# Hybrid conv and S5 block on one core: early activation table and TensorE work, broadcasts in transpose mode, another order for the last tile

## The chip, the core and the metric

The kernel runs as one program on one core of a Trainium2 chip. The metric is the device time of one execution in microseconds; three executions are shown. The core has TensorE (matmuls, PE in the profile; its weight loads are PEld), VectorE (DVE), ScalarE (ACT), GpSimd (POOL) and SyncE (SP), whose queue issues all transfers here. Each engine works through its own list in order; semaphores tie the lists together.

## What is computed

One decoder layer on a 1024 x 1024 float32 input, cut to what matters here:

```python
h = rms_norm(x, pre_g)
proj = h @ w_in                       # conv_a, conv_b, z_c, u_s, z_s, g_c, g_s
cu = ca * sigmoid(cb)
cu = causal_depthwise_conv(cu, conv_w, conv_b)          # 31 taps
cu = silu(layer_norm(cu, conv_ln_g, conv_ln_b))         # over the 1024 channels
conv_out = (cu * silu(z_c)) @ w_conv_out
y = gelu(s5_mimo(u_s, ...))                             # 32 groups, scan over time
y = y * sigmoid(y @ w_glu + b_glu)
ssm_out = (y * silu(z_s)) @ w_ssm_out
merged = sigmoid(g_c) * conv_out + sigmoid(g_s) * ssm_out
x_out = x + rms_norm(merged @ w_out, post_g)
```

## The kernel before

Activations lie with channels on partitions and the 1024 tokens along the free axis, in tiles of 128 x 1024. Each large product is done in three passes for accuracy: weights and activations are split into a high and a low part (`wh`, `wl`, `xh`, `xl`), and high x high, high x low and low x high are added up in PSUM. One output tile of a product over 1024 channels is therefore 8 x 3 x 2 = 48 matmuls of 128 x 512. ScalarE makes the high part, VectorE the low part.

**Start.** The product for u_s (`usp`, L852) begins on x that is not yet normalised: for each k-tile ScalarE multiplies x with the gain column (`gcol`) into `xh` and VectorE makes `xl` (L142, L143). The row scales are worked out beside it: ScalarE squares eight x tiles with a running sum (`xin`, L155), VectorE adds the epsilon, GpSimd raises to the power -0.5 (`r8t`, L159, 128 x 8). To use the scales along the free axis, `x_spread` (L163) spreads each of the eight columns of `r8t` over 128 columns and multiplies by the identity on TensorE into `rb`. That stands between the passes of k-tile 6 of `usp`. ScalarE copies it to `rbc`, with which x and the u_s results are scaled afterwards.

**Middle.** A list `seq` fixes the order of the products: `cb`/`ca` pairs feed the convolution, `gc`, `zc`, `zs`, `gs` are gates, `glu`, `so`, `co` the products of the two branches. Around them a planner (class `Clock`) places the rest while the program is built: every k-step of a product advances a clock by 1.296, and tasks written as generators (`yield cost, delay`) are taken up when their due time and VectorE's planned free time have come. The planned times set only the order in each engine's list. Tasks are the S5 branch, the convolution on VectorE (`conv_taps`, L539), per channel tile the transposes `lnp` with statistics `st` (`ln_stat`, L578 and L582), and `ln_chain`: after the eighth tile's statistics it forms the LayerNorm scale and shift per token (`lnr8`), spreads both over 128 columns by TensorE (`lnr`, `lnm`, L609), and then for each of eight tiles VectorE multiplies and adds (L622, L623), ScalarE applies Silu (L624), and VectorE multiplies by the reloaded z tile `zcr` (L617). In between ScalarE evaluates the gates: `gst` (L962) is the Sigmoid of a `gs` product and frees the PSUM buffer that holds it; `mm` products have two such buffers, the transposes have two of another tag (`aux`).

**End.** `out_k` (L1028) forms the output for eight groups of 128 tokens. `out_tail` squares the result on ScalarE with a running sum (L1043), multiplies it with the post gain on VectorE (L1044), forms the scale (L1047, L1048, GpSimd's power L1051), and adds x (L1055). The last group is done in two halves of 512.

Of the kernel before, what the change touches and what calls it, by code (L numbers as in the profile page):

```python
# [8 lines left out]
F32 = mybir.dt.float32  # L9
# [4 lines left out]
RMS_EPS = 1e-6  # L14
# [21 lines left out]
def tile_hybrid_block(  # L36
# [43 lines left out]
    def PS(name, tag):  # L80
        return ps.tile([128, 1024], F32, tag=tag, name=name)
# [25 lines left out]
    V.memset(mhalf, -0.5)  # L107
    V.memset(halfpi, math.pi / 2)

    xraw = {}  # L110

    def load_xt(k):
# [47 lines left out]

    def x_spread(rb):
        for t in range(8):
            PE.matmul(rb[:, t * 128:(t + 1) * 128], lhsT=r8t[:, t:t + 1].to_broadcast([128, 128]), rhs=ident,  # L163
                      start=True, stop=True)
        rbc = T("rbc")
        A.activation(out=rbc, in_=rb, func=AF.Copy)
        return rbc
# [404 lines left out]
    stat_left, ln_done = [8], [False]  # L572

    def ln_stat(c):
        yield 0.0, 3.5
        p = PS(f"lnp{c}", "aux")
        for t in range(8):
            PE.transpose(p[:, t * 128:(t + 1) * 128], acc[c][:, t * 128:(t + 1) * 128], ident)  # L578
        clk.now += 0.9
        yield 0.0, 2.0  # L580
        for t in range(8):
            V.bn_stats(out=st8[:, t, c, :], in_=p[:, t * 128:(t + 1) * 128])  # L582
            if t % 4 == 3:
                yield 0.9, 0.0
        stat_left[0] -= 1
        yield 0.0, 0.0
# [7 lines left out]
    def ln_chain():  # L594
# [11 lines left out]
        spread = [PS(f"ln{n}", "aux") for n in "rm"]  # L606
        for i, p in enumerate(spread):
            for t in range(8):
                PE.matmul(p[:, t * 128:(t + 1) * 128], lhsT=lnr8[:, i, t:t + 1].to_broadcast([128, 128]),  # L609
                          rhs=ident, start=True, stop=True)  # L610
        clk.now += 3.6
        zload(0)
        zload(1)
        yield 0.0, 3.0
# [112 lines left out]
    def js(j):  # L727
        return slice(j * 512, (j + 1) * 512)
# [72 lines left out]
    dmt = T("dmt")[0:16, 0:512].rearrange("p (g h) -> p g h", g=32)  # L801
    clk.now = clk.dve = 0.0
    usp = {m: PS(f"usp{m}", "aux" if m == 2 else "mm") for m in range(3)}
    for k in range(2):
        x_raw(k)
        us_split(0, k, 2)
# [226 lines left out]

    xo = {}

    def out_tail(pj, t):
        o = T(f"o{t}")
        q = T(f"q{t}")
        n = 1024 // len(pj)
        ssq = small.tile([128, 2], F32, tag="ossq", name=f"ossq{t}")  # L1040
        for i, p in enumerate(pj):
            s = slice(i * n, (i + 1) * n)
            A.activation(out=q[:, s], in_=p, func=AF.Square, accum_out=ssq[:, i:i + 1])  # L1043
            V.tensor_tensor(out=o[:, s], in0=p, in1=pog[:, s], op=ALU.mult)  # L1044
        v = small.tile([128, 1], F32, tag="ov", name=f"ov{t}")
        if len(pj) > 1:
            V.tensor_tensor(out=v, in0=ssq[:, 0:1], in1=ssq[:, 1:2], op=ALU.add)  # L1047
        V.tensor_scalar(out=v, in0=v if len(pj) > 1 else ssq[:, 0:1], scalar1=1.0 / 1024, scalar2=RMS_EPS,  # L1048
                        op0=ALU.mult, op1=ALU.add)
        r = small.tile([128, 1], F32, tag="rstd", name=f"orstd{t}")  # L1050
        G.tensor_tensor(out=r, in0=v, in1=mhalf[:, 0:1], op=ALU.pow)  # L1051
        xt = xo.pop(t)
        for i in range(len(pj)):
            s = slice(i * n, (i + 1) * n)
            V.scalar_tensor_tensor(out=o[:, s], in0=o[:, s], scalar=r, in1=xt[:, s], op0=ALU.mult, op1=ALU.add)  # L1055
            nc.sync.dma_start(out=ov[t][:, s], in_=o[:, s])
# [18 lines left out]
    for j in range(2):  # L1075
        for k in range(8):
            out_k(pl[j], 7, k, (j,))
    out_tail([pl[j][:, js(j)] for j in range(2)], 7)


VERBOSE = False
NT = 21
WRAW = 2
WHL = 2

_INS = ["x", "xt", "w_us", "w_in", "w_co", "w_glu", "w_so", "w_out", "pre_g", "post_g", "conv_w", "chan",
        "bglu", "lam", "bmat", "cmat", "dmat", "ident", "cst", "iota"]
# [67 lines left out]
```

## Time and profile before

| | us |
|---|---|
| median of three runs | 835.36 (834.99 to 835.5) |
| profiled execution | 834.89 |
| its span | 833.1 |
| TensorE matmuls busy | 816.3 (98%) |
| TensorE weight loads busy | 678.2 |
| VectorE busy | 622.6 (75%) |
| ScalarE busy | 279.4 (34%) |
| GpSimd busy | 26.4 (3%) |

A row of the timeline gives start and duration in microseconds, engine, line, operation, what it writes and reads, and how many like it were merged; in brackets stands how long the engine had been idle before and what ended that. Buffer numbers are left out of names. A matmul's duration contains its way through the array, so the pace of TensorE is read from one start to the next, not from durations. Waits of engines that nobody waits for cost nothing.

### The profile page before, as it was taken

To read this page: it belongs to the slowest core of one execution; us is meant where nothing else is said; L and a number is where in the kernel's file an instruction comes from. 1 tells how busy PE (TensorE), PEld (TensorE's weight loads), DVE (VectorE), ACT (ScalarE), POOL (GpSimd) and SP (SyncE) were. 2 spreads that over 40 slices of the span, in tenths; PEclk is the share of its full clock that TensorE was granted. 3 is DMA by queue.
4 is the path that set the end of the run, shared out by engine and by line. 5 is a ranking of instruction groups with operands and counts; after the bars stand their busy time and mean duration, and the time that the engine had idled before them with its cause. 6 is when DMAs were issued, how large, how long until landed. Compare 5 with 4: busy or idle time off the path is not lost.

```text
span 833.1 us, 9759 instructions
## 1 busy us (share of the span) xinstructions
PE 816.3 (98%) x3856; PEld 678.2 (81%) x3856; DVE 622.6 (75%) x902; ACT 279.4 (34%) x301; POOL 26.4 (3%) x26
## 2 busy tenths in 40 slices
PE   6999999999999999999999999999999999999996
PEld 5888888888888888888878888888878788888885
DVE  4689899896998899998989779397594644442242
ACT  5771624455325534323321131222254311122121
POOL 3400000000000000000000000000100000000010
PEclk9999999999999999999999999999999999999999
DMA  9703533533333112111112213122351644424142
GB/s 338 285 27 127 152 100 87 143 105 91 102 90 110 55 51 89 51 50 52 39 39 76 89 39 104 48 89 89 127 190 63 227 152 151 151 75 178 51 177 101
DMA packets 35180, 90.77 MB, mean 109 GB/s; under 512 B 8304, under 2 KB 13040, under 8 KB 35136
## 3 DMA queue, kind: packets, MB, share of 16 engines
q1 hardware_dynamic: 35136, 90.17, 32.2%
q8 instruction: 30, 0.49, 0.2%
q14 instruction: 14, 0.11, 0.0%
HBM read 65.90 MB, written 18.87 MB: 102 GB/s over the span
## 4 chain that ended last, share of the span: by engine, by line
PE 76%; DVE 16%; issue 3%; ACT 2%; DMA 2%; POOL 1%; SPq 0%; DVEq 0%; POOLq 0%; ACTq 0%
PE pgc L738 11%; PE pco L738 10%; PE po L1028 10%; PE pgs L738 9%; PE pcb L738 8%; PE pzc L738 8%; PE pca L738 8%; DVE pp L539 6%; PE pso L738 4%; DVE acc L539 3%; PE usp L871 1%; PE pgl L738 1%; DMA xt<-in_xt_dram 1%; DMA xin<-in_x_dram 1%; POOL spt L227 1%
## 5 line engine op out<-in xcount | busy, mean ns | idle before, releaser
L539 DVE SCALAR_TENSOR_TENSOR pp<-ext,cw,pp 128x512 f32<-128x512 f32 x232 | 165.6, 745 | 9.9 <-ACT pp L530 9.8
L539 DVE SCALAR_TENSOR_TENSOR acc<-ext,hs,acc 128x512 f32<-128x512 f32 x120 | 89.3, 744 | 0.0
L1028 PE MATMUL po<-wox,mgh 128*128 128x512 f32 x192 | 52.3, 389 | 0.0
L1028 PEld LDWEIGHTS po<-wox,mgh 128*128 128x128 f32 x192 | 36.0, 188 | 7.5
L738 PE MATMUL pgs<-xh,wh_gs 128*128 128x512 f32 x128 | 39.6, 391 | 1.2 <-ACT gst L962 1.2
L515 ACT ACTIVATE ext<-ext 128x1179 f32<-128x1179 f32 x8 | 9.5, 1191 | 92.7 <-DVE ext L514 92.7
L738 PE MATMUL pgc<-xh,wh_gc 128*128 128x512 f32 x128 | 40.6, 398 | 0.0
L738 PE MATMUL pca<-xh,wh_ca 128*128 128x512 f32 x128 | 40.1, 395 | 0.0
L738 PE MATMUL pzc<-xh,wh_zc 128*128 128x512 f32 x128 | 39.9, 393 | 0.0
L1000 DVE TENSOR_TENSOR sgr<-pco,sgr 128x1024 f32<-128x1024 f32 x8 | 9.8, 1224 | 40.1 <-PE pco L738 40.1
L738 PE MATMUL pca<-xh,wl_ca 128*128 128x512 f32 x128 | 39.6, 390 | 0.0
L1044 DVE TENSOR_TENSOR o<-po,postg 128x1024 f32<-128x1024 f32 (+1 forms) x9 | 10.0, 1106 | 39.6 <-ACT q L1043 39.6
L738 PE MATMUL pco<-cuh,wl_co 128*128 128x512 f32 x128 | 39.5, 390 | 0.0
L738 PE MATMUL pcb<-xh,wh_cb 128*128 128x512 f32 x128 | 39.5, 390 | 0.0
L738 PE MATMUL pca<-xl,wh_ca 128*128 128x512 f32 x128 | 39.5, 389 | 0.0
L738 PE MATMUL pgc<-xl,wh_gc 128*128 128x512 f32 x128 | 39.5, 390 | 0.0
L738 PE MATMUL pzc<-xh,wl_zc 128*128 128x512 f32 x128 | 39.5, 389 | 0.0
L738 PE MATMUL pzc<-xl,wh_zc 128*128 128x512 f32 x128 | 39.5, 389 | 0.0
L738 PE MATMUL pgc<-xh,wl_gc 128*128 128x512 f32 x128 | 39.5, 389 | 0.0
L738 PE MATMUL pgs<-xl,wh_gs 128*128 128x512 f32 x128 | 39.4, 389 | 0.0
L738 PE MATMUL pco<-cuh,wh_co 128*128 128x512 f32 x128 | 39.4, 389 | 0.0
L738 PE MATMUL pcb<-xl,wh_cb 128*128 128x512 f32 x128 | 39.4, 389 | 0.0
(267 smaller groups left out, 1799.9 us busy)
## 6 DMA issues: line engine op xcount, KB each, us to landing
xt<-in_xt_dram SPq DMA_DIRECT2D x8, 512.0 KB, 6.1
xin<-in_x_dram SPq DMA_DIRECT2D x8, 512.0 KB, 9.8
wr_cb<-in_w_in_dram SPq DMA_DIRECT2D x8, 512.0 KB, 3.4
wr_ca<-in_w_in_dram SPq DMA_DIRECT2D x8, 512.0 KB, 3.3
wr_gc<-in_w_in_dram SPq DMA_DIRECT2D x8, 512.0 KB, 3.7
gc_scratch<-gct SPq DMA_DIRECT2D x8, 512.0 KB, 2.7
wr_zc<-in_w_in_dram SPq DMA_DIRECT2D x8, 512.0 KB, 3.3
zc_scratch<-zct SPq DMA_DIRECT2D x8, 512.0 KB, 2.6
```

Source lines behind the costliest of these rows:

```text
L227: G.tensor_tensor(out=r[:, g_], in0=ebase2[:, g_], in1=a[:, g_], op=ALU.pow)
L515: A.activation(out=ext[:, :, 0:3, 1:132], in_=ext[:, :, 4:7, 0:131], func=AF.Copy)
L539: V.scalar_tensor_tensor(out=o, in0=src(e, r), scalar=w, in1=o, op0=ALU.mult, op1=ALU.add)
L738: PE.matmul(p[:, js(j)], lhsT=lhs[:, ks], rhs=rhs(k, j), start=st, stop=sp_)
L871: PE.matmul(usp[3][:, js(j)], lhsT=lhs[:, ks], rhs=rhs[:, k, js(j)], start=st, stop=sp_)
L1000: V.tensor_tensor(out=sgt, in0=p, in1=sgt, op=ALU.mult)
L1028: PE.matmul(p[:, js(j)], lhsT=lhs[k][:, s], rhs=rhs[k][:, js(j)], start=st, stop=sp_)
L1044: V.tensor_tensor(out=o[:, s], in0=p, in1=pog[:, s], op=ALU.mult)
```

## The change

- A one-column ScalarE copy to `scrap` stands first in ScalarE's list; it reads only a constant, so the activation table is loaded ahead of it and not ahead of the first split.
- VectorE fills a tile `warm`, and TensorE runs three (`WARM`) float32 matmuls on it into a PSUM buffer that nobody reads.
- The broadcasts of `r8t` and of `lnr8` (scale and shift) use TensorE's transpose instead of a product with the identity. The planner counts 1.8 instead of 3.6 for the LayerNorm ones, and the delay ahead of each tile's statistics is 5.0 instead of 3.5. Both move the tasks behind them.
- The last token group uses `out_last`: product with the gain ahead of the square in each half, and the mean of squares added up in two steps, the first on the first half.

```diff
--- before.py
+++ after.py
@@ -107,6 +107,9 @@
     V.memset(mhalf, -0.5)
     V.memset(halfpi, math.pi / 2)
 
+    scrap = small.tile([128, 1], F32, tag="scrap", name="scrap", bufs=1)
+    A.activation(out=scrap, in_=halfpi, func=AF.Copy)
+
     xraw = {}
 
     def load_xt(k):
@@ -160,8 +163,7 @@
 
     def x_spread(rb):
         for t in range(8):
-            PE.matmul(rb[:, t * 128:(t + 1) * 128], lhsT=r8t[:, t:t + 1].to_broadcast([128, 128]), rhs=ident,
-                      start=True, stop=True)
+            PE.transpose(rb[:, t * 128:(t + 1) * 128], r8t[:, t:t + 1].to_broadcast([128, 128]), ident)
         rbc = T("rbc")
         A.activation(out=rbc, in_=rb, func=AF.Copy)
         return rbc
@@ -572,7 +574,7 @@
     stat_left, ln_done = [8], [False]
 
     def ln_stat(c):
-        yield 0.0, 3.5
+        yield 0.0, 5.0
         p = PS(f"lnp{c}", "aux")
         for t in range(8):
             PE.transpose(p[:, t * 128:(t + 1) * 128], acc[c][:, t * 128:(t + 1) * 128], ident)
@@ -606,9 +608,8 @@
         spread = [PS(f"ln{n}", "aux") for n in "rm"]
         for i, p in enumerate(spread):
             for t in range(8):
-                PE.matmul(p[:, t * 128:(t + 1) * 128], lhsT=lnr8[:, i, t:t + 1].to_broadcast([128, 128]),
-                          rhs=ident, start=True, stop=True)
-        clk.now += 3.6
+                PE.transpose(p[:, t * 128:(t + 1) * 128], lnr8[:, i, t:t + 1].to_broadcast([128, 128]), ident)
+        clk.now += 1.8
         zload(0)
         zload(1)
         yield 0.0, 3.0
@@ -801,6 +802,11 @@
     dmt = T("dmt")[0:16, 0:512].rearrange("p (g h) -> p g h", g=32)
     clk.now = clk.dve = 0.0
     usp = {m: PS(f"usp{m}", "aux" if m == 2 else "mm") for m in range(3)}
+    warm = T("warm")
+    V.memset(warm[:, 0:640], 0.0)
+    pw_ = PS("warm", "aux")
+    for _ in range(WARM):
+        PE.matmul(pw_[:, 0:512], lhsT=warm[:, 512:640], rhs=warm[:, 0:512], start=True, stop=True)
     for k in range(2):
         x_raw(k)
         us_split(0, k, 2)
@@ -1033,6 +1039,25 @@
 
     xo = {}
 
+    def out_last(pj, t):
+        o, q = T(f"o{t}"), T(f"q{t}")
+        ssq = small.tile([128, 2], F32, tag="ossq", name=f"ossq{t}")
+        v = small.tile([128, 1], F32, tag="ov", name=f"ov{t}")
+        xt = xo.pop(t)
+        for i, p in enumerate(pj):
+            V.tensor_tensor(out=o[:, js(i)], in0=p, in1=pog[:, js(i)], op=ALU.mult)
+            A.activation(out=q[:, js(i)], in_=p, func=AF.Square, accum_out=ssq[:, i:i + 1])
+            if i == 0:
+                V.tensor_scalar(out=v, in0=ssq[:, 0:1], scalar1=1.0 / 1024, scalar2=RMS_EPS, op0=ALU.mult,
+                                op1=ALU.add)
+        V.scalar_tensor_tensor(out=v, in0=ssq[:, 1:2], scalar=1.0 / 1024, in1=v, op0=ALU.mult, op1=ALU.add)
+        r = small.tile([128, 1], F32, tag="rstd", name=f"orstd{t}")
+        G.tensor_tensor(out=r, in0=v, in1=mhalf[:, 0:1], op=ALU.pow)
+        for i in range(2):
+            V.scalar_tensor_tensor(out=o[:, js(i)], in0=o[:, js(i)], scalar=r, in1=xt[:, js(i)], op0=ALU.mult,
+                                   op1=ALU.add)
+            nc.sync.dma_start(out=ov[t][:, js(i)], in_=o[:, js(i)])
+
     def out_tail(pj, t):
         o = T(f"o{t}")
         q = T(f"q{t}")
@@ -1075,13 +1100,14 @@
     for j in range(2):
         for k in range(8):
             out_k(pl[j], 7, k, (j,))
-    out_tail([pl[j][:, js(j)] for j in range(2)], 7)
+    out_last([pl[j][:, js(j)] for j in range(2)], 7)
 
 
 VERBOSE = False
 NT = 21
 WRAW = 2
 WHL = 2
+WARM = 3
 
 _INS = ["x", "xt", "w_us", "w_in", "w_co", "w_glu", "w_so", "w_out", "pre_g", "post_g", "conv_w", "chan",
         "bglu", "lam", "bmat", "cmat", "dmat", "ident", "cst", "iota"]
```

The planner's numbers move work on three engines. On TensorE, the LayerNorm broadcasts stand inside the last `zc` product in the kernel before (the last `pzc`; `pgs` is the `gs` product behind it):

```order
L738 MATMUL pzc_4365<-xh,wh_zc_4313 128x512 x2
L738 MATMUL pzc_4365<-xl,wh_zc_4313 128x512 x2
L738 MATMUL pzc_4365<-xh,wl_zc_4330 128x512 x2
L609 MATMUL lnr<-ident,lnr_99 128x128 x8
L609 MATMUL lnm<-ident,lnr_99 128x128 x8
L738 MATMUL pzc_4365<-xh,wh_zc_4313 128x512 x2
L738 MATMUL pzc_4365<-xl,wh_zc_4313 128x512 x2
L738 MATMUL pzc_4365<-xh,wl_zc_4330 128x512 x2
L738 MATMUL pzc_4365<-xh,wh_zc_4313 128x512 x2
L738 MATMUL pzc_4365<-xl,wh_zc_4313 128x512 x2
L738 MATMUL pzc_4365<-xh,wl_zc_4330 128x512 x2
L738 MATMUL pgs_4466<-xh,wh_gs_4399 128x512 x2
```

and in the changed kernel:

```order
L739 MATMUL pzc_4369<-xh,wl_zc_4338 128x512 x2
L739 MATMUL pzc_4369<-xh,wh_zc_4321 128x512 x2
L739 MATMUL pzc_4369<-xl,wh_zc_4321 128x512 x2
L739 MATMUL pzc_4369<-xh,wl_zc_4338 128x512 x2
L611 MATMUL lnr<-ident,lnr_101 128x128 x8
L611 MATMUL lnm<-ident,lnr_101 128x128 x8
L739 MATMUL pgs_4468<-xh,wh_gs_4399 128x512 x2
L739 MATMUL pgs_4468<-xl,wh_gs_4399 128x512 x2
L739 MATMUL pgs_4468<-xh,wl_gs_4421 128x512 x2
```

They now stand behind all matmuls of that product, twelve matmuls later.

On ScalarE, the same stretch before, from the last rows ahead of the Silus (`acc`) to the Sigmoid `gst` of the next `gs` product and the table load behind it:

```order
L624 ACTIVATE acc_823<-acc_823,chn 128x1024
L624 ACTIVATE acc_1466<-acc_1466,chn 128x1024
L932 ACTIVATE zct_4482<-pzc_4365 128x1024
L624 ACTIVATE acc_2227<-acc_2227,chn 128x1024
L705 ACTIVATE wh_so_4494<-wr_so_4332 128x512
L624 ACTIVATE acc_2590<-acc_2590,chn 128x1024
L624 ACTIVATE acc_2906<-acc_2906,chn 128x1024
L705 ACTIVATE wh_gs_4549<-wr_gs_4417 128x1024
L962 ACT_TABLE_LOAD
L962 ACTIVATE gst_4551<-pgs_4466 128x1024
L624 ACT_TABLE_LOAD
```

and in the changed kernel:

```order
L625 ACTIVATE acc_831<-acc_831,chn 128x1024
L938 ACTIVATE zct_4484<-pzc_4369 128x1024
L706 ACTIVATE wh_so_4493<-wr_so_4340 128x512
L625 ACTIVATE acc_1474<-acc_1474,chn 128x1024
L625 ACTIVATE acc_2235<-acc_2235,chn 128x1024
L625 ACTIVATE acc_2598<-acc_2598,chn 128x1024
L706 ACTIVATE wh_gs_4551<-wr_gs_4423 128x1024
L968 ACT_TABLE_LOAD
L968 ACTIVATE gst_4553<-pgs_4468 128x1024
L625 ACT_TABLE_LOAD
L625 ACTIVATE acc_2914<-acc_2914,chn 128x1024
```

Further on in the changed kernel, with the two last `gst`:

```order
L625 ACTIVATE acc_3322<-acc_3322,chn 128x1024
L625 ACTIVATE acc_3698<-acc_3698,chn 128x1024
L968 ACT_TABLE_LOAD
L968 ACTIVATE gst_4668<-pgs_4583 128x1024
L625 ACT_TABLE_LOAD
L625 ACTIVATE acc_4066<-acc_4066,chn 128x1024
L706 ACTIVATE wh_so_4679<-wr_so_4572 128x512
L968 ACT_TABLE_LOAD
L968 ACTIVATE gst_4717<-pgs_4652 128x1024
L706 ACTIVATE wh_so_4728<-wr_so_4626 128x512
L990 ACTIVATE cuh<-acc_831 128x1024
```

Four Silus instead of five stand ahead of the first `gst`, `wh_so` stands ahead of the second Silu instead of behind the third, and the eighth Silu now stands between the two last `gst`, with a table load on either side of it. On SP the load of the third z tile (`zcr`) moves behind the last store of `zct`.

On TensorE at the end of the fifth `ca` product to be followed by `gs`, the transposes for the statistics of three tiles before:

```order
L738 MATMUL pca_3174<-xh,wh_ca_3129 128x512 x2
L738 MATMUL pca_3174<-xl,wh_ca_3129 128x512 x2
L738 MATMUL pca_3174<-xh,wl_ca_3146 128x512 x2
L578 MATMUL lnp_3239<-ident,acc_2227 128x128 x8
L738 MATMUL pca_3174<-xh,wh_ca_3129 128x512 x2
L738 MATMUL pca_3174<-xl,wh_ca_3129 128x512 x2
L738 MATMUL pca_3174<-xh,wl_ca_3146 128x512 x2
L578 MATMUL lnp_3262<-ident,acc_2590 128x128 x8
L578 MATMUL lnp_3279<-ident,acc_2906 128x128 x8
L738 MATMUL pgs_3288<-xh,wh_gs_3199 128x512 x2
L738 MATMUL pgs_3288<-xl,wh_gs_3199 128x512 x2
```

and in the changed kernel:

```order
L739 MATMUL pca_3182<-xl,wh_ca_3137 128x512 x2
L739 MATMUL pca_3182<-xh,wl_ca_3154 128x512 x2
L580 MATMUL lnp_3247<-ident,acc_2235 128x128 x8
L739 MATMUL pca_3182<-xh,wh_ca_3137 128x512 x2
L739 MATMUL pca_3182<-xl,wh_ca_3137 128x512 x2
L739 MATMUL pca_3182<-xh,wl_ca_3154 128x512 x2
L580 MATMUL lnp_3270<-ident,acc_2598 128x128 x8
L739 MATMUL pgs_3287<-xh,wh_gs_3207 128x512 x2
L739 MATMUL pgs_3287<-xl,wh_gs_3207 128x512 x2
L739 MATMUL pgs_3287<-xh,wl_gs_3227 128x512 x2
L580 MATMUL lnp_3294<-ident,acc_2914 128x128 x8
L739 MATMUL pgs_3287<-xh,wh_gs_3207 128x512 x2
```

The third group of transposes, which had followed the second directly, now stands six matmuls into `pgs`; at the three later tiles the transposes also stand six matmuls later.

## Rows read from the trace of the kernel before

**Rows 1.** The busy line of the profile's page: busy us (share of span) xinstructions

```profile
PE 816.3 (98%) x3856; PEld 678.2 (81%) x3856; DVE 622.6 (75%) x902; ACT 279.4 (34%) x301; POOL 26.4 (3%) x26
```

**Rows 2.** TensorE's waits in the whole span: us in total, times, longest

```profile
PE lnp L578 <- DVE st L582: 0.7, 2, 0.5
```

**Rows 3.** Timeline of the start: start, duration, engine, line, what, count, idle before

```profile
4.31 1.28 ACT L142 ACT_TABLE_LOAD   x1 [4.31 <-DMA gcol<-in_pre_g_dram]
...
5.61 1.15 ACT L142 ACTIVATE xh<-xt,gcol 128x1024 fp32r<-128x1024 f32 x1
...
7.22 2.93 PE L852 MATMUL usp<-xh,wush 128*128 128x512 f32 x6 [7.22 <-ACT wush L132]
...
11.67 1.52 PE L852 MATMUL usp<-xl,wush 128*128 128x512 f32 x6
...
13.03 1.52 PE L852 MATMUL usp<-xh,wush 128*128 128x512 f32 x6
```

**Rows 4.** Timeline, the way to the row scales and their broadcast

```profile
24.33 1.06 ACT L155 ACTIVATE xin<-xin 128x1024 f32<-128x1024 f32 x1 [0.55 <-DMA xin<-in_x_dram]
...
33.24 1.28 DVE L143 SCALAR_TENSOR_TENSOR xl<-xt,gcol,xh 128x1024 fp32r<-128x1024 f32 x1
...
34.75 1.66 POOL L159 TENSOR_TENSOR r8t<-ssq,mhalf 128x8 f32<-128x8 f32 x1 [3.82 <-DVE spt L251]
34.79 1.52 PE L852 MATMUL usp<-xh,wusl 128*128 128x512 f32 x6
...
36.47 2.05 PE L163 MATMUL rb<-ident,r8t 128*128 128x128 f32 x16 [0.15 <-POOL r8t L159]
...
38.27 1.63 PE L852 MATMUL usp<-xl,wush 128*128 128x512 f32 x6
```

**Rows 5.** Timeline, VectorE at two joints with TensorE: after row scaling, ahead of glu

```profile
46.96 1.22 DVE L176 TENSOR_TENSOR xl<-xt,xh 128x1024 fp32r<-128x1024 f32 x1 [2.17 <-ACT xh L175]
...
288.70 4.63 DVE L794 TENSOR_TENSOR yl<-y,yh 128x1024 fp32r<-128x1024 f32 x4 [1.57 <-ACT yh L793]
```

**Rows 6.** Timeline, eight transposes of channel tile 7 and what follows on TensorE

```profile
583.54 1.03 PE L578 MATMUL lnp<-ident,acc 128*128 128x128 f32 x8
...
584.34 0.70 PE L738 MATMUL pzc<-xh,wh_zc 128*128 128x512 f32 x2
```

**Rows 7.** Timeline, LayerNorm broadcasts and the chain to the next free PSUM buffer

```profile
593.97 1.95 PE L609 MATMUL lnr<-ident,lnr 128*128 128x128 f32 x16
...
595.95 1.22 DVE L622 TENSOR_TENSOR acc<-lnr,acc 128x1024 f32<-128x1024 f32 x1 [4.70 <-PE lnr L609]
...
597.45 0.71 PE L738 MATMUL pzc<-xh,wh_zc 128*128 128x512 f32 x2
597.74 1.23 DVE L623 TENSOR_TENSOR acc<-lnm,acc 128x1024 f32<-128x1024 f32 x1 [0.56 <-PE lnm L609]
...
606.71 0.69 DVE L713 TENSOR_TENSOR wl_so<-wr_so,wh_so 128x512 fp32r<-128x512 f32 x1 [0.70 <-ACT wh_so L705]
...
609.83 1.25 ACT L624 ACTIVATE acc<-acc,chn 128x1024 f32<-128x1024 f32 x1 [3.15 <-DVE acc L623]
...
613.35 1.25 ACT L624 ACTIVATE acc<-acc,chn 128x1024 f32<-128x1024 f32 x1 [2.28 <-DVE acc L623]
...
616.86 1.02 ACT L962 ACTIVATE gst<-pgs 128x1024 f32<-128x1024 f32 x1
...
617.93 0.73 PE L738 MATMUL pgs<-xh,wh_gs 128*128 128x512 f32 x2 [1.16 <-ACT gst L962]
...
640.02 1.03 ACT L962 ACTIVATE gst<-pgs 128x1024 f32<-128x1024 f32 x1 [8.59 <-PE pgs L738]
```

**Rows 8.** Timeline, the end of the last tile

```profile
826.36 0.60 ACT L1043 ACTIVATE q<-po 128x512 f32<-128x512 f32 x1 [4.69 <-PE po L1028]
...
827.08 0.69 DVE L1044 TENSOR_TENSOR o<-po,postg 128x512 f32<-128x512 f32 x1 [4.69 <-ACT q L1043]
...
828.17 0.54 POOL L1051 TENSOR_TENSOR orstd<-ov,mhalf 128x1 f32<-128x1 f32 x1 [9.53 <-DVE ov L1048]
```

## The prediction

> **What bounds the kernel now.** I read four views, in this order. The busy line of the page comes first [rows 1]: TensorE's matmuls are busy 816.3 of the span's 833.1 us, no other engine over 75%. Next TensorE's own waits [rows 2]: apart from the 7.22 us before its first matmul [rows 3], its largest is 1.16 us for one PSUM buffer [rows 7], then 0.7 us in two waits at transposes. So the end is set by the sum of TensorE's instructions plus a few short waits, and a saving counts only if it shortens that stream or one of those waits. Third, the timeline of the start and of the row scales [rows 3, 4], which shows who else could hold TensorE back early. Fourth, the same view where the LayerNorm chain feeds back [rows 7] and at the end [rows 8]. Where VectorE is late it was itself released by TensorE: at 46.96 it had idled 2.17 us for ScalarE, at 288.70 1.57 us [rows 5]. A stream that is about 1 us earlier therefore pulls VectorE along at both joints.
>
> The profiled execution took 834.89 us, 1.79 more than its span. The sum is made against it; the median shown, 835.36, is 0.47 higher, and I add that at the end.
>
> **Start: table load and clock.** ScalarE's table load waits for the gain column until 4.31, and the first split starts 1.30 us later, at 5.61; with the table there it may start at 4.31 at the earliest [rows 3]. The first x tile must also have landed, which no row dates more closely than 5.61, so TensorE starts 0 to 1.3 us earlier. From 7.22 to 13.03 it ran three groups of six matmuls; a later group takes 13.03 - 11.67 = 1.36 us, so 5.81 us stand where 4.08 would: 1.73 us lost to starting at half pace, 1.2 instead of 2.4 GHz, after 7.22 us of nothing [rows 3]. The three added matmuls run while the loads do; at worst they end after the first split and take some of the 1.3 back. VectorE's added fill stands ahead of its first use of data. Together TensorE could be 1.30 + 1.73 = 3.0 us ahead.
>
> I put all of it at nothing, because of what is late next. The row-scale broadcast stands in TensorE's queue between the passes of k-tile 6, and everything on TensorE is queued behind it. It needs r8t, which GpSimd ends at 34.75 + 1.66 = 36.41 [rows 4]. TensorE is ready for it at 34.79 + 1.36 = 36.15 now, and would be at 33.1. The chain to r8t does not move: the squares resume at 24.33 when an x load lands, ScalarE and then VectorE's in-order split at 33.24 follow, then GpSimd [rows 4], and none of these waits for TensorE. The loads are issued at the same places, behind VectorE work that itself waits for later x tiles. So TensorE's head start becomes a wait of 36.41 - 33.1 = 3.3 us.
>
> The Trainium skill (ScalarE: Activation LUTs, What ACT_TABLE_LOAD costs) puts a switch of tables at 2.66 us, drain included. The trace has 1.30 from the start of the load to the next activation [rows 3]. By the page the head start would be 4.4 us instead of 3.0 and be lost in the same wait.
>
> **Row-scale broadcast.** Eight full-precision products, 16 records, take 38.27 - 36.47 = 1.80 us of TensorE [rows 4]. Eight transposes of the same size take 584.34 - 583.54 = 0.80 [rows 6]. They stand on the path, since they start when r8t is there: gain 1.0. The nearest rows have a full tile as operand, not a repeated column; bounds 0 (the repeated column costs as now) and 1.1.
>
> **LayerNorm broadcasts.** The same exchange twice: 597.45 - 593.97 = 3.48 becomes 1.6, gain 1.9, bounds 0 and 2.0 [rows 6, 7].
>
> **What moves behind them.** The broadcasts now stand at the end of the last zc product, 12 matmuls or 2.72 us further on in TensorE's order, so in the old run's time they would start at 593.97 + 2.72 = 596.69. What hangs on them is the chain VectorE, ScalarE's Silu, table load, Sigmoid of gst, which frees the PSUM buffer of the next gs product. Before, that chain took 616.86 - 593.97 = 22.89 and TensorE waited 1.16 at 617.93 [rows 7]. Now four instead of five tiles pass ahead of gst: 613.35 - 609.83 = 3.52 less. The transposes are done 1.04 instead of 1.98 after their start (1.03 busy in rows 6): 0.94 less. VectorE's wait for the second broadcast, 0.56, goes, and so does its 0.70 for wh_so, which ScalarE now does ahead of the second tile instead of behind the third [rows 7]. That leaves 17.17: gst starts at 613.86 and TensorE is released 1.07 later, as in the rows, at 614.93. It arrives at 616.77 - 1.88 = 614.89. The wait shrinks from 1.16 to about 0: gain 1.1. If the 0.70 stays, the gain is 0.5; if the chain keeps its old length, TensorE waits 620.65 - 614.89 = 5.8 us, 4.6 more than now. On SP the load of the third z tile moves behind the last store of zc, which ScalarE frees near 602.5 by the same additions; the third tile's gate comes some 7 us later, and if the load took longer, VectorE and all behind it would stand. I take 1.1, since each subtraction is an instruction that is no longer ahead. Two more table loads, 1.30 us each by rows 3, and the eighth tile, 3.52, now stand on ScalarE between the two last gst; ahead of the last one it had idled 8.59 us [rows 7], which covers these 6.1. Without that cover the splits cuh, queued behind it, would be late for the next stage.
>
> **Transposes for the statistics.** Four tiles' transposes stand six matmuls later. The first of them had stood right behind another tile's and waited 0.5 us, the longer of the two waits in rows 2, until VectorE's statistics freed a PSUM buffer; now 1.36 us of matmuls stand between, more than that wait: gain 0.5, bounds 0 and 0.5. Its own statistics slip behind the next tile's convolution, and what they hold is a PSUM buffer that the transposes after next want, so nothing waits for them.
>
> **Last tile.** Before, square and product follow each other: 0.72 us from 826.36 to 827.08, then 1.09 to GpSimd [rows 8]. Now the product goes first, and I let the square wait for it, as the product waited for the square, though neither needs the other's result: both read the same half of PSUM [rows 8]. 0.69 for the product, some 0.05 to hand over, 0.72 for the square, about 0.30 for one small operation instead of two: 1.76 against 1.81. Gain 0.05, bounds -0.2 and 0.7 (both at once).
>
> **Sum.** 1.0 + 1.9 + 1.1 + 0.5 + 0.05 = 4.55. 834.89 - 4.55 = 830.3, or 830.8 beside the median.
>
> **Rivals.** *The clock falls in the new wait.* TensorE would idle 3.3 us ahead of the broadcast. The trace has two such rows: after 1.16 us idle it went on at full pace (two matmuls in 0.73 us), after 7.22 us it began at half pace [rows 3, 7]. 3.3 lies nearer the first. If it falls, the 1.73 us of the start are paid here, and up to 0.8 for the transposes: 830.8 + 2.1 = 832.9. In the Trainium skill, TensorE: Matmul & The Clock Gate (Why this matters for your kernels) counts idle gaps between bursts of matmuls among the things that return the array to its lower clock; by it this rival is the likelier one, and no row here settles a gap of this length. Chance 0.25.
>
> *The head start is kept*: the way to r8t moves with TensorE after all, say because ScalarE's split of the third weight tile, which waits for TensorE, comes earlier. Against it: a load ends ScalarE's idle time after that. 830.8 - 3.0 = 827.8. Chance 0.06.
>
> *The transposes are no faster* because the repeated column costs as it does now: 830.8 + 2.9 = 833.7. For it: no row shows such an operand in a transpose. Chance 0.05.
>
> *Slower: the clock falls in that wait and stays down.* TensorE runs one remaining pass, three passes and the fourth us product at half pace, 1.36 + 4.08 + 10.9 (eight groups of six) = 16.3 us of work, and loses as much again: 830.8 + 16.3 = 847.1. It decides from 4.55 us of work at half pace on; against it the first start regained full pace after two groups [rows 3]. Chance 0.04.
>
> **Numbers.** The forecast has 0.60 and its own range is 829.7 to 831.9 (buffer wait, tail). 829.2 to 833.0 adds most of the clock case and leaves out the kept head start, the slow cases and the edges. A difference under 0.2% (1.7 us) can't be told from none here. Faster: forecast, clock case, head start and little of the fourth, 0.88 after some is left for what I did not see; same 0.08; slower 0.04.
>
> **What would show it.** Right: TensorE starts near 6, at full pace from its second group at the latest, then waits about 3 us for r8t, which still ends near 36.4; rb, lnr and lnm show 8 records each and some 0.8 us; the wait on gst is under 0.7 and the longer wait at lnp is gone. Wrong: matmuls 0.45 us apart after rb (the clock); r8t ending near 33 (the head start kept); 16 records for rb; a wait of over 1.2 us on gst, which would mean that the LayerNorm chain, now started later, has become the bound there.

## The result, and the profile after

The changed kernel takes 831.26 us (median of six executions, 830.1 to 831.91), the kernel before, timed beside it, 835.43 (834.99 to 835.75): ratio 0.995, 95% interval 0.9937 to 0.9962. Timed again later it took 831.44 against 835.36, ratio 0.9959 (0.9946 to 0.9972). The forecast was 830.8. The total is right to 0.5 us, and one of the steps under it is not. One execution of a kernel further down (the held kernel) took 910.23 us at a granted clock of 0.851 and stands in none of the figures.

The profiled execution of the kernel after took 831.63 us, its span is 829.9 (before 834.89 and 833.1). The busy line and TensorE's waits (in total, times, longest), from the page and the view of the waits; three more, of 0.4 us and less, are as long as before:

```profile
PE 818.3 (99%) x3838; PEld 677.4 (82%) x3838; DVE 622.6 (75%) x903; ACT 282.1 (34%) x304; POOL 25.4 (3%) x26
```

```profile
PE rb L166 <- POOL r8t L162: 2.2, 1, 2.2
PE warm L809 <- DVE warm L806: 1.6, 1, 1.6
PE lnp L580 <- DVE st L584: 0.2, 1, 0.2
```

Beside [rows 1, 2]: TensorE is still what bounds the kernel. It has 24 instructions fewer in the broadcasts and 6 more for warming, and is busy for 2.0 us more: the warming runs from 1.65 to 6.93, when TensorE was idle before, and some later instructions took longer, as the rows below show. The wait on gst is gone from the list, the waits at lnp fell from 0.7 to 0.2, and at the top stands a wait of 2.2 us for r8t.

The start, from the timeline (start, duration, engine, line, what, count, idle before), answers to [rows 3]. The rows of one window merge differently in another, so the last pass of the warming and the first matmul of usp are shown by themselves behind the groups that hold them:

```profile
0.73 1.28 ACT L111 ACT_TABLE_LOAD   x1 [0.73 <-PEq L1169]
...
4.31 1.15 ACT L145 ACTIVATE xh<-xt,gcol 128x1024 fp32r<-128x1024 f32 x1 [2.08 <-DMA gcol<-in_pre_g_dram]
...
1.65 5.28 PE L809 MATMUL warm<-warm 128*128 128x512 f32 x6 [1.65 <-DVE warm L806]
6.14 2.17 PE L858 MATMUL usp<-xh,wush 128*128 128x512 f32 x6
8.16 1.53 PE L858 MATMUL usp<-xh,wusl 128*128 128x512 f32 x6
...
6.07 0.86 PE L809 MATMUL warm<-warm 128*128 128x512 f32 x1
6.14 1.02 PE L858 MATMUL usp<-xh,wush 128*128 128x512 f32 x1
```

The table is loaded while ScalarE would idle, and xh starts at 4.31 instead of 5.61, the full 1.30. TensorE starts 7.22 - 6.14 = 1.08 earlier. Its first group takes 8.16 - 6.14 = 2.02, not the 1.36 of a group at full pace, and the second group is at full pace. Nearly all of the 0.66 between them lies ahead of the group's second matmul: the sixth pass of the warming begins only at 6.07, and the first matmul behind it lasts 1.02 where one of its kind lasts 0.39 at full pace; the other five follow 0.23 apart. So here the warming itself is in the way of the first product. All in all the pass ahead of the broadcast starts at 32.64 instead of 34.79: a lead of 2.15 us.

What became of the lead, the same view, answers to [rows 4]; the last row is the first matmul of the fourth us product, and the fence behind it has two rows of the kernel before:

```profile
32.64 1.52 PE L858 MATMUL usp<-xh,wusl 128*128 128x512 f32 x6
...
34.62 1.66 POOL L162 TENSOR_TENSOR r8t<-ssq,mhalf 128x8 f32<-128x8 f32 x1 [3.81 <-DVE spt L253]
...
36.34 1.09 PE L166 MATMUL rb<-ident,r8t 128*128 128x128 f32 x8 [2.17 <-POOL r8t L162]
37.18 2.79 PE L858 MATMUL usp<-xl,wush 128*128 128x512 f32 x6
39.77 1.99 PE L858 MATMUL usp<-xh,wush 128*128 128x512 f32 x6
41.59 1.53 PE L858 MATMUL usp<-xh,wusl 128*128 128x512 f32 x6
...
44.33 0.62 PE L877 MATMUL usp<-xh,wh_us 128*128 128x512 f32 x2
```

```profile
39.74 1.54 PE L852 MATMUL usp<-xh,wush 128*128 128x512 f32 x6
...
43.84 0.61 PE L871 MATMUL usp<-xh,wh_us 128*128 128x512 f32 x2
```

GpSimd ends r8t at 36.28, before at 36.41: that chain did not move, and the lead became a wait. The transposes take 37.18 - 36.34 = 0.84, the products took 1.80. Then two groups take 39.77 - 37.18 = 2.59 and 41.59 - 39.77 = 1.82 instead of 1.36 each: 1.69 us more. Some 0.1 of that stands behind every broadcast (the first group behind it took 39.74 - 38.27 = 1.47 before), so close to 1.6 us are lost. The row of the stretch shows why (stretch, length, then busy time with its count for PE, PEld, DVE, ACT and POOL, the granted clock, the transfer engines' share, GB/s):

```profile
37.20:40.80 3.60, 3.60 (x12) 2.86 (x10) 3.42 (x13) 1.18 (x2) 0.00 (x0) 0.53 0.33 116
```

The granted clock is 0.53 from 37.2 to 40.8, the lower of its two levels (1.2 GHz) but for the edges; ahead of it TensorE had idled 2.17 us. So in this execution TensorE stands 44.33 - 43.84 = 0.49 us later than before at the fourth product, with the cheaper broadcast in it.

The statistics' transposes and the LayerNorm chain, answering to [rows 2, 6, 7]; the first fence is the kernel before:

```profile
422.78 1.09 PE L578 MATMUL lnp<-ident,acc 128*128 128x128 f32 x8 [0.17 <-DVE st L582]
424.36 1.09 PE L578 MATMUL lnp<-ident,acc 128*128 128x128 f32 x8 [0.49 <-DVE st L582]
...
616.16 0.61 PE L738 MATMUL pso<-y2h,wl_so 128*128 128x512 f32 x2
```

```profile
423.20 1.09 PE L580 MATMUL lnp<-ident,acc 128*128 128x128 f32 x8 [0.15 <-DVE st L584]
...
596.40 1.04 PE L611 MATMUL lnr<-ident,lnr 128*128 128x128 f32 x8
597.27 1.04 PE L611 MATMUL lnm<-ident,lnr 128*128 128x128 f32 x8
...
610.10 1.25 ACT L625 ACTIVATE acc<-acc,chn 128x1024 f32<-128x1024 f32 x1 [2.28 <-DVE acc L624]
...
613.61 1.03 ACT L968 ACTIVATE gst<-pgs 128x1024 f32<-128x1024 f32 x1
...
614.03 0.61 PE L739 MATMUL pso<-y2h,wl_so 128*128 128x512 f32 x2
614.68 0.74 PE L739 MATMUL pgs<-xh,wh_gs 128*128 128x512 f32 x2
...
636.82 1.03 ACT L968 ACTIVATE gst<-pgs 128x1024 f32<-128x1024 f32 x1 [3.56 <-PE pgs L739]
```

The two broadcasts take 598.06 - 596.40 = 1.66 us (the next matmul starts at 598.06) instead of 3.48. The fourth Silu is the last ahead of gst, which starts at 613.61, 17.21 us after the first broadcast (17.17 and 613.86 were worked out). Between the last pair of pso, 0.45 long, and the next gs product stand 614.68 - 614.03 - 0.45 = 0.20 us; counted the same way it was 617.93 - 616.16 - 0.45 = 1.32 before, and not the 1.16 of [rows 7], where idling counts from the pair's modelled end. The idle time ahead of the last gst is 3.56, before 8.59: the cover held.

The last tile, answering to [rows 8]:

```profile
822.75 0.39 PE L1034 MATMUL po<-wox,mgl 128*128 128x512 f32 x1
...
823.18 0.69 DVE L1048 TENSOR_TENSOR o<-po,postg 128x512 f32<-128x512 f32 x1 [3.79 <-PE po L1034]
823.90 0.60 ACT L1049 ACTIVATE q<-po 128x512 f32<-128x512 f32 x1 [4.70 <-DVE o L1048]
...
824.93 0.54 POOL L1055 TENSOR_TENSOR orstd<-ov,mhalf 128x1 f32<-128x1 f32 x1 [9.46 <-DVE ov L1053]
```

The square starts when the product ends: one still waits for the other. GpSimd starts 824.93 - 822.75 = 2.18 after the last matmul starts, before 828.17 - 825.93 = 2.24 by this row and [rows 8]:

```profile
825.93 0.39 PE L1028 MATMUL po<-wox,mgl 128*128 128x512 f32 x1
```

The account of this execution from TensorE's starts: +0.49 up to the fourth product; then up to lnr -0.78 (596.40 against 593.97 + 2.72 = 596.69, which is -0.29 in all); from there to the last matmul -2.89 (825.93 became 822.75, -3.18 in all); the tail -0.06. The sum, -3.24, is the change of the span.

### The profile page after: what moved, and what is told of

Its sections match the earlier page's. It is cut to its first block, busy times and chain, and to the rows that moved or that the text cites. A ratio compares the mean times of both kernels' runs of the same rounds, so it can differ in the third digit from the quotient of the medians.

```text
span 829.9 us, 9728 instructions
## 1 busy us (share of the span) xinstructions
PE 818.3 (99%) x3838; PEld 677.4 (82%) x3838; DVE 622.6 (75%) x903; ACT 282.1 (34%) x304; POOL 25.4 (3%) x26
## 4 chain that ended last, share of the span: by engine, by line
PE 78%; DVE 14%; DMA 3%; issue 2%; ACT 2%; SPq 0%; POOL 0%; DVEq 0%; POOLq 0%; ACTq 0%
PE pgc L739 11%; PE pgs L739 11%; PE pco L739 11%; PE po L1034 10%; PE pzc L739 8%; PE pcb L739 8%; PE pca L739 8%; DVE pp L541 6%; PE pso L739 5%; DVE acc L541 3%; DMA xt<-in_xt_dram 1%; PE usp L877 1%; DMA xin<-in_x_dram 1%; PE pgl L739 1%; PE ep L415 1%
## 5 line engine op out<-in xcount | busy, mean ns | idle before, releaser
L739 PE MATMUL pco<-cul,wh_co 128*128 128x512 f32 x128 | 39.4, 389 | 0.0
L739 PE MATMUL pgs<-xh,wl_gs 128*128 128x512 f32 x128 | 39.4, 389 | 0.0
L739 PE MATMUL pcb<-xh,wl_cb 128*128 128x512 f32 x128 | 39.4, 389 | 0.0
```

The costliest lines, as they stand in the source:

```text
L739: PE.matmul(p[:, js(j)], lhsT=lhs[:, ks], rhs=rhs(k, j), start=st, stop=sp_)
```

## Experiments

Theory W: the head start ends in the wait for r8t, and the low clock behind the broadcast comes of that wait. Its rivals are named in each expectation; the main ones are N (the clock falls for another reason) and H (the head start brings something). Four kernels went first, beside the kernel before (835.2).

**The broadcast later in TensorE's order.** The changed kernel with one line altered:

```
-            if k == 6 and n_ == 5:
+            if k == 7 and n_ == 2:
                 rbc = x_spread(PS("rb", "aux"))
```

The lines below it in the same block, which set the planner's account of VectorE and record the row scalings, move with it.

> The row-scale broadcast stands six pairs of matmuls (2.72 us) later in TensorE's order, in k-tile 7 instead of 6; all else is as in the changed kernel. Theory W (the head start of 2.15 us ends in the wait for r8t, and the lower clock that follows comes of that wait): TensorE gets to the broadcast at 34.0 + 2.72 = 36.7, after r8t at 36.3, so no wait over 0.2 us, granted clock 1.00 from 36 to 42, and the fourth us product starts near 40.5 instead of 44.33. The 3.8 us are kept unless VectorE's split chain (idle 2.8 us at 47.45) becomes late: 827.5 to 829.5, best guess 828.3. Rival N (the lower clock comes of the transposes or of chance, not of the wait): the clock still falls to 0.5 behind the broadcast, and only the wait goes: about 829.2. Rival D (VectorE's chain sets the time here anyway): waits of the same length appear at the convolution products, 831.

Measured 835.07 (833.78 to 836.14), ratio 0.9997 (0.9988 to 1.0006): the whole gain gone. At the broadcast all went as W said: no wait, clock 1.00, fourth product at 40.55. The rows show where it was lost, on TensorE and on VectorE (39.80 in the kernel after for the second row):

```profile
57.63 1.22 PE L739 MATMUL pcb<-xh,wl_cb 128*128 128x512 f32 x2 [5.14 <-DVE wl_cb L714]
...
44.58 4.86 DVE L172 SCALAR_TENSOR_TENSOR xt<-xt,gcol,rbc 128x1024 f32<-128x1024 f32 x4
```

The planner fills VectorE with S5 chores until the row scalings are recorded, so the 2.72 us that they came later let it put some 4 us of chores (40.44 to 44.58) ahead of them. wl_cb came late, TensorE waited 5.14 us, and behind that wait the clock fell as well: the pair that starts at 57.63 takes 1.02 us instead of 0.45. No theory had this in its numbers: the edit moved more than the broadcast.

**Without the warming matmuls** (the fill and the three matmuls left out, the early table load kept).

> The changed kernel without the three warming matmuls and their fill; the early table load stays. Theory W: the first matmul starts near 6.1 at half pace and three groups take 5.8 us, so about 0.8 us less of lead than with warming: the wait for r8t is 1.3 instead of 2.17 us. If a wait of that length leaves the clock alone (as 1.16 us did before), the time is 831.3 - 1.7 = 829.6; if the clock falls as well, 831.3. Rival N (clock falls by chance or by the transposes): 831.3 whatever the wait. Rival H (warming is what brings the gain): 833 or more.

Measured 830.36 (829.75 to 830.78), ratio 0.9941 (0.9929 to 0.9954). The row of the broadcast and that of the clock:

```profile
36.99 1.09 PE L166 MATMUL rb<-ident,r8t 128*128 128x128 f32 x8 [2.00 <-POOL r8t L162]
```

```profile
37.20:40.80 3.60, 3.60 (x21) 3.09 (x20) 3.38 (x18) 1.85 (x2) 0.00 (x0) 1.00 0.10 24
```

r8t ended at 36.94 in this execution, so the wait was 2.00 and not 1.3, and yet the clock stayed at 1.00. A wait of 2.0 us can thus pass without a fall, so neither W nor N is decided here. Rival H is out: nothing is lost without warming.

**Transposes and planner numbers alone** on the kernel before, with neither of the two head edits nor the new tail.

> The kernel before with the transposes for both broadcasts and the two planner numbers alone: no early table load, no warming, the old tail. Theory W: the broadcast waits only the 0.3 us that it waited before, the clock stays at 1.00, and the time is the kernel before less 1.0 (rb), 2.9 (LayerNorm) and 0.7 (statistics), 835.4 - 4.6 = 830.8 or less, so not slower than the changed kernel. Rival H (the early table load and the warming are worth something): 832 or more. Rival N: the clock falls behind rb here too, 832.4.

Measured 830.57 (830.16 to 832.1), ratio 0.9947 (0.9934 to 0.9961): not told apart from the whole change. This part carries all of the gain; 835.2 - 830.57 = 4.6 stands beside a forecast of 4.5 for it.

**The two head edits alone** on the kernel before.

> The kernel before with the early table load and the three warming matmuls alone. Theory W: 2 us of lead turn into a wait of 2.2 us for r8t, and the matmuls behind it run at half pace for 1.7 us of loss (a little more, as the eight broadcast products are in it): 835.4 + 1.7 to 2.5 = 837 to 838 where the clock falls, 835.4 where it doesn't. Rival H (head start of use): 833.3. Rival N (the transposes bring the clock down): 835.4, clock at 1.00 behind rb.

Measured 836.14 (834.54 to 837.31), ratio 1.0011 (1.0002 to 1.002): slightly slower than the kernel before. In the profiled execution:

```profile
36.04 2.66 PE L166 MATMUL rb<-ident,r8t 128*128 128x128 f32 x16 [1.90 <-POOL r8t L162]
...
38.36 2.72 PE L860 MATMUL usp<-xl,wush 128*128 128x512 f32 x6
40.91 1.53 PE L860 MATMUL usp<-xh,wush 128*128 128x512 f32 x6
```

```profile
37.20:40.80 3.60, 3.60 (x15) 3.12 (x14) 3.28 (x12) 1.02 (x1) 0.00 (x0) 0.53 0.41 125
```

The wait and the fall are there with products instead of transposes, so the transposes are not their cause. The loss is 38.36 - 36.04 - 1.80 = 0.52 in the products and 40.91 - 38.36 - 1.47 = 1.08 in the group behind them, 1.6 in all. The size expected, 1.7 to 2.5 on the median, was too much: of eleven executions two kept a mean granted clock of 0.998 or more and took 834.54 and 835.31.

These four left open whether the wait itself brings the clock down, and whether the head start can be had at all. Four more kernels:

**The wait filled with work:** eight matmuls of no use between the pass and the broadcast.

```
             if k == 6 and n_ == 5:
-                rbc = x_spread(PS("rb", "aux"))
+                rb = PS("rb", "aux")
+                for _ in range(8):
+                    PE.matmul(rb[:, 0:512], lhsT=h[:, kk[0]], rhs=xh[:, k, 0:512], start=True, stop=True)
+                rbc = x_spread(rb)
```

> The changed kernel with eight more matmuls of a us weight (0.227 us each at full pace, 1.8 us in all; their result is overwritten) between the second pass of k-tile 6 and the broadcast, so TensorE works through the wait for r8t instead of idling. Theory W (the low clock behind the broadcast comes of TensorE idling there): idle time ahead of rb under 0.5 us, granted clock 1.00 from 36 to 42, the fourth us product starts at 42.7 instead of 44.3, and the time is 831.3 - 1.4 = 829.9 (the executions of the changed kernel in which the clock does not fall gain nothing, so less than the full 1.7). Rival N (the clock falls for another reason): the fall stays, and the eight matmuls cost nothing or up to 0.3 us: 831.3.

Measured 830.15 (829.66 to 831.05), ratio 0.9941 (0.9929 to 0.9953), all five executions at a mean granted clock of 0.997 or 0.998.

```profile
36.54 1.09 PE L166 MATMUL rb<-ident,r8t 128*128 128x128 f32 x8 [0.54 <-POOL r8t L162]
37.38 1.62 PE L858 MATMUL usp<-xl,wush 128*128 128x512 f32 x6
38.84 1.52 PE L858 MATMUL usp<-xh,wush 128*128 128x512 f32 x6
```

Same point of the program, same wait for r8t, but TensorE works through it: the group behind it takes its 1.46, no fall. The median is 1.3 us below that of the changed kernel timed beside it (831.44), with eight matmuls more whose result is thrown away. The two ranges overlap (829.66 to 831.05 against 829.77 to 833.73), so the gain in time is likely and not certain; N would have it only by chance.

**The broadcast later, VectorE's account held.**

```
             if k == 6 and n_ == 5:
+                clk.dve = max(clk.dve, clk.now + 1.5) + 4 * 1.28
+            if k == 7 and n_ == 2:
                 rbc = x_spread(PS("rb", "aux"))
-                clk.dve = max(clk.dve, clk.now + 1.5)
+                held = clk.dve
                 for k_ in range(4):
                     x_scale(k_, rbc)
+                clk.dve = held
```

> The broadcast six pairs of matmuls later in TensorE's order, as in the cover run, but with the planner's account of VectorE left as in the changed kernel, so that VectorE's and ScalarE's orders do not change. Theory V (the cover run lost its 3.8 us because the planner used the later broadcast to put 4 us of S5 chores ahead of the four row scalings on VectorE, which made wl_cb late): the scalings start at 39.8 to 40.3 instead of 44.6, ScalarE's copies of the us products start near 40, wl_cb is split near 52.5, TensorE's wait for it is under 1 us instead of 5.1, and the time is 827.6 to 829, best guess 828.3: the fastest so far. Rival D (VectorE's stream cannot be earlier here whatever its order): the wait for wl_cb stays at 3 us and over, and the time is 831 or more.

Measured 828.89 (four executions, 828.55 to 830.16), ratio 0.9927 (0.9915 to 0.994).

```profile
53.45 0.73 PE L739 MATMUL pcb<-xh,wl_cb 128*128 128x512 f32 x2 [0.61 <-DVE wl_cb L714]
```

```profile
40.40 4.87 DVE L172 SCALAR_TENSOR_TENSOR xt<-xt,gcol,rbc 128x1024 f32<-128x1024 f32 x4
...
52.18 1.22 DVE L714 TENSOR_TENSOR wl_cb<-wr_cb,wh_cb 128x1024 fp32r<-128x1024 f32 x1
```

Theory V by its numbers: scalings at 40.40, wl_cb at 52.18, its wait 0.61 instead of 5.14. Six us lie between this kernel and the first of this section, and the two differ only in where the chores stand on VectorE.

**The planner's old numbers** (3.5 and 3.6 put back, transposes kept).

> The changed kernel with the planner's two old numbers (3.5 for the statistics' transposes, 3.6 for the broadcasts); the transposes stay. By the terms of the prediction the wait on the gst buffer (1.1) and the longer wait at the statistics' transposes (0.5; 0.7 by the trace after) come back: 831.3 + 1.7 = 833.0. Rival P (the placement is worth nothing, the waits went because the transposes are shorter): 831.3, with no wait over 0.4 at pgs or lnp.

Measured 834.06 (832.79 to 835.76), ratio 0.9985 (0.9976 to 0.9993).

```profile
PE lnp L580 <- DVE st L584: 0.7, 2, 0.5
```

```profile
614.74 0.61 PE L739 MATMUL pso<-y2h,wl_so 128*128 128x512 f32 x2
617.00 0.74 PE L739 MATMUL pgs<-xh,wh_gs 128*128 128x512 f32 x2 [1.64 <-ACT gst L968]
```

Both waits are back, and the one on gst, 1.64, is longer than the 1.16 before [rows 7]: TensorE comes to it sooner by more than the shorter broadcasts save on the chain to gst. From start to start it is 617.00 - 614.74 - 0.45 = 1.81, against 0.20 in the changed kernel, and the late group of transposes again stands 1.58 behind the one ahead of it. So of the 3.7 us that the trace of the changed kernel gains here (0.78 and 2.89), the planner's two numbers hold more than half: 1.61 at gst and 0.78 at lnp, 2.4 in all. The two profiled executions, both with the fall, differ by 833.99 - 831.63 = 2.36.

**The changed kernel again.**

> The changed kernel once more, beside the three others of this call. All theories: 830.1 to 831.9. Theory W adds: an execution with a wait of about 2 us for r8t has a granted clock of 0.5 for some 3 us behind the broadcast and the fourth us product at 44 or later, one without has it at 42.7.

Median 831.44 (829.77 to 833.73). Its profiled execution took 830.04:

```profile
36.29 1.09 PE L166 MATMUL rb<-ident,r8t 128*128 128x128 f32 x8 [1.74 <-POOL r8t L162]
...
42.69 0.62 PE L877 MATMUL usp<-xh,wh_us 128*128 128x512 f32 x2
```

```profile
37.20:40.80 3.60, 3.60 (x18) 2.98 (x17) 3.42 (x13) 1.13 (x2) 0.00 (x0) 1.00 0.26 102
```

No fall here, with nearly the same wait, and the fourth product at 42.69 instead of 44.33. The changed kernel's executions look to be of two kinds. Of all twelve, six have a mean granted clock of 0.996 or less and took 831.1 to 833.7 (mean 832.2), six have 0.997 or more and took 829.8 to 831.4 (mean 830.5). The difference, 1.7 us, is near what the two traces show: from rb to the fourth product 44.33 - 36.34 = 7.99 with the fall and 42.69 - 36.29 = 6.40 without, 1.59 more. But only these two of the twelve have a trace, and the mean also holds a low clock that every profiled execution shows behind its last matmul (0.50 from 826.8 on in both). The profiled execution of the head edits alone fell at a mean of 0.997. So the count of six and six is likely, not certain.

Last, whether the length of the wait decides, the tail, and how far the head start carries:

**The broadcast three pairs earlier**, a longer wait (x_spread at `k == 6 and n_ == 2`, the scalings where they were).

> The changed kernel with the broadcast three pairs of matmuls (1.36 us) earlier in TensorE's order, the other engines' orders as they were: TensorE idles about 3.5 us ahead of it instead of 1.7 to 2.2, and all behind it ends 1.36 later. Theory W (the longer TensorE idles there, the surer the clock falls): every execution has the fall, 832.6 (the slower of the two groups of the changed kernel's executions) + 1.4 = 834.0. Rival L (length does not matter): still two groups, 831.6 and 834, median 832.8. Rival N (no link with idling): 831.4 + 1.4 = 832.8 in one group, clock at 1.00.

Measured 832.65 (831.11 to 833.83), ratio 0.9965 (0.9952 to 0.9977).

```profile
36.08 1.09 PE L166 MATMUL rb<-ident,r8t 128*128 128x128 f32 x8 [2.88 <-POOL r8t L162]
36.92 1.64 PE L858 MATMUL usp<-xh,wusl 128*128 128x512 f32 x6
```

W, as I had put it, fails here: the profiled execution (831.16) waited 2.88 us and went on at full pace. Two executions at 0.998 took 831.1, three at 0.996 to 0.997 took 832.7 to 833.8, as rival L has it; the median alone fits N's 832.8 as well. Between 1.7 and 2.9 us the length of the wait does not settle whether the clock falls.

**The old last tile** in the changed kernel (`out_tail` instead of `out_last`).

> The changed kernel with the old last tile (square ahead of product). All theories: same time as the changed kernel within 0.1 us by the trace: GpSimd's power starts 2.24 us behind the last matmul instead of 2.18. Rival B (product and square run together once the product goes first): the old tail is 0.7 us slower, 832.1.

Measured 831.73 (830.14 to 832.46), ratio 0.9961 (0.9947 to 0.9975), the changed kernel's time. By the trace GpSimd starts 823.35 - 821.12 = 2.23 after the last matmul starts, instead of 2.18. Rival B is out.

**The held kernel without warming.**

> The held cover run without the three warming matmuls. Theory W (a head start is worth its length once nothing behind it waits): TensorE gets to the broadcast 0.8 us later than with warming (first matmul at half pace until 10), so 829.1 + 0.8 less the 0.4 to 0.6 us by which the wait for wl_cb shrinks: 829.3 to 829.9. Rival H (warming brings nothing even here, since the wait for wl_cb is what ends last): 829.1, and the wait for wl_cb gone.

Measured 829.54 (828.83 to 829.67), ratio 0.9929 (0.9917 to 0.9942): not told apart from the held kernel with warming. The wait for wl_cb (0.6 in the held kernel) is gone from its waits, so part of the lead that the warming had brought only goes into that wait there.

**The held kernel with wl_cb split one k-tile earlier.**

```
         if k == 1:
             wsplit_h()
-        if k == 2:
             wsplit_l()
```

> The held cover run with the split of wl_cb one k-tile earlier on VectorE (ahead of the third xl). Theory V: the 0.6 us wait for wl_cb goes and nothing replaces it: 829.1 - 0.5 = 828.6, the fastest. Rival D (VectorE's stream ends last whatever its order): another xl or the same split is waited for as long, 829.1.

Measured 827.83 (827.69 to 828.22), ratio 0.9911 (0.9898 to 0.9925): the fastest kernel of the study, 3.4 to 3.6 us below the changed one. wl_cb is split at 49.99, the matmul that waited for it runs at 52.56 without a wait, and the broadcast waits 0.51 us for r8t; no fall in the profiled execution, and a mean granted clock of 0.998 or 0.999 in all four.

## Why the prediction was right, step by step

**Row-scale broadcast**, 1.0: 1.80 - 0.84 = 0.96. The repeated column costs a transpose nothing.

**LayerNorm broadcasts and the wait on gst**, 1.9 and 1.1: 3.48 - 1.66 = 1.82 and, from start to start, 1.32 - 0.20 = 1.12; 2.94 together, 2.89 in the account of starts. That subtracting what no longer stands ahead of gst gave 17.17 us for 17.21 is the best-working step of the text. The run with the old numbers shows that the wait would have grown from 1.16 to 1.64 had the broadcasts not been moved too.

**Statistics**, 0.5: 0.78. The profile put 0.5 down as idle, but from start to start the late group in the kernel before stood 424.36 - 422.78 = 1.58 behind the one ahead of it, 0.78 more than the 0.80 that it takes [rows 6]. An idle figure counts from a modelled end; starts do not.

**Last tile**, 0.05: 0.06 in the profiled execution, and the run with the old tail agrees. The square does wait for the product.

**Start**, "I put all of it at nothing". This is the step that was off, by its size. The argument held up to the wait: r8t did not move, and the lead was lost there. The lead was 2.15, not 3.0: TensorE started 1.08 earlier and not 1.30, and the last pass of the warming held up the first group by 0.66, which the text had thought possible and not counted. But nothing is not what it cost. In about half of the executions the clock seems to have fallen behind the wait, for 1.6 us; in the profiled one the text's own sign of it, matmuls 0.45 us apart behind rb, is there (six in 2.59). That is the rival "the clock falls in the new wait" (0.25, 2.1 us, 832.9): by the mean granted clock it came true in six executions of twelve at 832.2, the forecast in the other six at 830.5. The median stands between the two, so 830.8 came out close partly by luck; the five terms of the sum measured 4.74 against 4.55. The head edits alone cost 0.9 us (0.2 to 1.7 by the interval).

That the fall follows TensorE's idling is what all fourteen profiled executions agree on: the granted clock fell behind three waits for r8t, at the end of the 5.14 us wait for wl_cb and behind the last matmul, and nowhere else. What decides in which executions it falls in the wait for r8t is not shown. The length does not: falls came after 1.90, 2.17 and 2.34 us, none after 1.74, 1.77, 2.00 and 2.88. The clock records of the traces order these seven by the moment at which the clock had risen in the start: 6.57, 6.60 and 6.18 us with a fall, 7.34, 7.07, 9.10 and 7.43 without. In all three falls the clock went down 30.72 us after it had risen, but 1.25, 0.97 and 0.61 us after the wait had ended: the fall keeps its distance from the rise, not from the wait. In the profiled execution with the filled wait the clock had risen at 6.63, close to the three with a fall, and it did not fall. The Trainium skill (TensorE: Matmul & The Clock Gate, What's actually happening) says that the chip judges activity in a rhythm of its own that does not begin anew with a kernel. These rows agree with that, and no run here shifts that rhythm by itself, so it is not shown that it decides.

**What the prediction didn't see:** a lead need not be lost. The broadcast's place was taken as given. Put six pairs of matmuls (2.72 us) later, with VectorE's chores held, it has more than the lead's length of work ahead of it, and with one split moved the kernel takes 827.8. That this is also the number of the rival "the head start is kept" (830.8 - 3.0) is chance: the lead measured 2.15 and not 3.0, and it was kept by a way that the text did not have.

## What to carry to other kernels

When one engine's start is made earlier, look for the first operand that does not come earlier with it: there the lead ends, and idling there can turn it into a loss, since the clock may fall behind it (0.9 us here). Work that needs nothing that is late belongs in that gap, and if a planner records the order, hold its other accounts still while one instruction is moved: the same move lost 3.6 us or gained 2.5 against the changed kernel (831.44) by where the chores of another engine went. An edit that removes time from one chain and moves another has two prices; timing each alone (transposes 4.6 us faster, head edits 0.9 slower) tells them, the total does not.

## What the hardware showed that was not expected

The granted clock fell in some executions and not in others of the same program at the same place, after idle times from 1.9 to 2.3 us, and came back while TensorE worked without a break. In the three profiled executions that fell there, the fall stood 30.72 us behind the rise of the clock in the start, and the rise came anywhere from 5.6 to 7.7 us in the profiled executions with warming. In the first microseconds the view of the granted clock reads 1.00 in both kernels, but in the kernel before the first six matmuls, from 7.22 to 9.95, take 2.73 us instead of 1.36. There the pace of the matmuls shows the clock; the record itself begins only with the rise, at 10.69. And r8t, which depends on loads and on nothing that was changed, ended between 35.99 and 37.02 in the profiled executions of all the kernels: a microsecond that goes into the time wherever TensorE waits for it. The last kernel, which hardly waits, spreads over 0.5 us in four executions, the changed one over 4 us in twelve.
